# A streaming encoder step on one core: the sample's value products beside the first prompt rows', other buffers and addresses for some weights, other column chunks

## The chip, the cores and the metric

The kernel runs on one core of a Trainium2 chip. Its engines are PE (matrix products; PEld is its weight load), DVE (vector), ACT (scalar, with activation functions), POOL (GpSimd) and SP (issues transfers). On-chip memory is SBUF; matrix products are accumulated in banks of PSUM. The time is microseconds (us) of one execution on the device. Lines such as L1385 are those of the kernel before; below the change they move by a few.

## What is computed

One inference step of an encoder layer, in float32, for 1024 prompt rows and 64 sample rows (the sample also has 512 cached rows of keys and values). One projection of width 6144 gives queries, keys, values and a gate z for two branches of eight heads of 64 each, and two output gates. The first branch ("sb") is stick-breaking attention, the second ("cb") softmax attention in a band with a relative bias. Cut to that:

```python
h = rms_norm(x, norm_w) @ w_in
sb_q, sb_k, sb_v, sb_z, cb_q, cb_k, cb_v, cb_z, g_sb, g_cb = jnp.split(h, SPLIT_POINTS, axis=-1)
# stick-breaking: suffix sums of log(1 - beta) over the keys behind
suffix = lax.cumsum(log_keep, axis=3, reverse=True) - log_keep
w = jnp.where(causal, jnp.exp(log_beta + suffix), 0.0)
o_sb = jnp.einsum("bhqk,bkhd->bqhd", w, v)
# band: keys of the own chunk of 64 and the eight before it
o_cb = softmax(q @ k * ATTN_SCALE + bias) @ v
b_sb = (o_sb * jax.nn.silu(sb_z)) @ w_proj_sb
b_cb = (o_cb * jax.nn.silu(cb_z)) @ w_proj_cb
y = x + (jax.nn.sigmoid(g_sb) * b_sb + jax.nn.sigmoid(g_cb) * b_cb) @ w_out
```

Prompt and sample go through the same formulas; y and the new keys and values of both are returned.

## The kernel before

Every float32 factor is split in two parts, high (rounded) and low (the rest), and a product is made of three: high by high, high by low, low by high. Where blocks of weights are multiplied with blocks of x, a scheme of seven products of sums in place of eight products is used on top of that. The order of all instructions is written out by hand (manual_schedule): each engine takes its own in program order, and semaphores that the framework sets between tiles make one engine wait for another. A tile of a pool with bufs=2 may be taken again only when all users of the tile two before are done.

The stages, one after another on PE:

- Natural products (L528, 11 to 177 us): six blocks of 256 columns, nine row tiles each. The weights of a half block are whi and wlo (pool wpool) or whix and wlox (pool natx); x and the sums of x are xa, xm, xb. In between DVE makes four sums of x, t0 to t3, each with a high and a low part (tiles t0h, t0l and so on) in jobs, one at each place (block, tile) of the list jobs_at; the operations are at L189. open_t allots t0 and t1 in the pool tp0, t2 and t3 in the pool tp2; pad puts unused bytes behind one of them. POOL and DVE also normalise and store; hl at L375 is the low part of transposed keys, for which PE's transposes pk at L370 wait.
- Pairs (L868, 218.6 to 516.1 us): 14 pairs of column blocks, each in seven steps s = 0 to 6 of 24 products into one of three banks for two chunks c of columns (256 and 288). The operands of a step are t0 to t3 or x, and a weight block that prep(n + LEAD), five steps before, has cast to its high part on ACT (L456) and whose low part POOL has made. Results are joined on DVE at L876 (u2, u3), L880 and L888 and emitted; s1 at L872 is ACT's copy of the first. A bank is written again only after DVE has read it. In pairs 0 and 2 keys are made: PE transposes them (L787, into acc) and ACT copies them out (ko, kos, L790 to L799); pairs 1 and 3 make queries (emitted by ACT as hl at L765, by DVE at L766).
- Units (run_fill, L1037): the output gates' columns, four plain units with three chunks of columns, 1088 in all (CH); they run from 516.1 us, and their rest and the projection of the first branch (L1144) fill gaps of the attention.
- Attention (540 to 812 us): eight passes (b, p), two heads each. A pass goes over t = 8 (the sample), 0, 1, ..., 7 (row tiles of 128). qk makes z = q k (L1293); for "sb" ACT takes the sigmoid (L1296) and DVE a scan (mid, L1315), for "cb" DVE adds the bias and takes a minimum (L1298) and ACT the exponential (L1306) and the scaling (L1318). Four rows of the sequence later tr transposes (L1346, pt), ACT or DVE copies to wT (L1355, L1357), and av(b, p, j) multiplies wT by the values into the PSUM tile o (L1385): vp for prompt rows, j = 0 to 3 (256 rows), vs for the sample, j = 4. Then DVE reads o and multiplies by the gate tile zt (L1394 for "sb", L1396 for "cb"), and POOL stores zt an iteration later. The pool of o has one buffer. The list avq holds when av is due.
- Branch and output projections (L1186, L1705, to 958 us).

The two places of the attention loop that set when av comes:

```python
        while avq and avq[0][0] <= i:
            av(*avq.pop(0)[1:])
...
            if t == 8 or hd == 1 and t % 2 == 1:
                avq.append((i + (3 if t == 8 else 2), b, p, t // 2 if t < 8 else 4))
```

Of the kernel before, what the change touches and what calls it, by code (L numbers as in the profile page):

```python
# [8 lines left out]
F32 = mybir.dt.float32  # L9
F32R = mybir.dt.float32r  # L10
# [23 lines left out]
def hybrid_step_kernel(ctx: ExitStack, tc: tile.TileContext, x_prompt, x_sample, c_sbk, c_sbv, c_cbk, c_cbv,  # L34
# [80 lines left out]
    class Weights:  # L115
# [18 lines left out]
        def lo(self, key, eng=None):  # L134
            raw, pool, shape, extra = self.raw.pop(key)
            h = self.sp[key][0]
            l = shifted(pool, shape, 1) if extra else pool.tile(shape, F32R, name="wlo", bufs=2)
            (eng or G).tensor_tensor(out=l, in0=raw, in1=h[:].bitcast(F32), op=OP.subtract)
            self.sp[key] = (h, l)
# [74 lines left out]
    with ExitStack() as ph:  # L214
# [219 lines left out]
        def prep(n):  # L434
# [14 lines left out]
            shape = [128, 2, 4, 128]  # L449
            if s in (0, 3):  # L450
                t = shifted(natx, shape, 1)
            elif s in (2, 4):
                t = natx.tile(shape, F32R, name="whix", bufs=2)
            else:
                t = wpool.tile(shape, F32R, name="whi" if s == 5 else "wlo", bufs=2)
            A.activation(t[:, 0], src, AF.Copy)  # L456
# [72 lines left out]
        tms = [None] * 4  # L529
        jobs_at = [(2, 0), (2, 3), (2, 6), (3, 0), (3, 4), (3, 7), (4, 1), (4, 4)]  # L530

        rb_at = [(1, 0), (1, 1), (1, 3), (1, 4), (1, 6), (1, 7), (2, 0), (2, 1)]

        def open_t(ns):
            tp = sx.enter_context(tc.tile_pool(name=f"tp{ns[0]}", bufs=1, side="right"))
            for n in ns:
                tms[n] = [tp.tile([128, 4, XO], F32R, name=f"t{n}{s}") for s in "hl"]
            if ns[0] == 0:
                pad(tp, 128)
# [463 lines left out]
    def ev_act(func, dst, ci, a, b, ps):  # L1003
        n = b - a
        sg = am.tile([128, 384], F32, name="sg", bufs=3)
        A.activation(sg[:, :n], ps[:, :n], func)
        for o, n0, m in pieces(a, b):
            store_later(dst[:, n0:n0 + m], sg[:, o:o + m])
# [21 lines left out]
    def run_fill():  # L1030
        for j, (kind, c, args) in enumerate(units):
            wh, wl = W.sp.pop(("u", j))
            for ci, (a, b) in enumerate(CH):
                ps = psF.tile([128, 512], F32, name="acc")
# [331 lines left out]
    def av(b, p, j):  # L1366
        o = psO.tile([128, 256], F32, name="o")
        vp, vs = VP[b, p]
# [89 lines left out]
    for i in range(len(seq) + LAG + 2):  # L1458
# [34 lines left out]
        if 0 <= i - LAG < len(seq):  # L1493
            tr(i - LAG)
            b, p, t, hd = seq[i - LAG]
            if t == 8 or hd == 1 and t % 2 == 1:
                avq.append((i + (3 if t == 8 else 2), b, p, t // 2 if t < 8 else 4))
        fill(m - m // 2)
# [299 lines left out]
```

## Time and profile before

| | |
|---|---|
| median of three runs | 962.02 us (960.46 to 962.95) |
| the profiled execution | 960.25 us |
| its span | 958.5 us, TensorE clock 0.999 |
| busy PE / DVE / ACT / POOL | 951.5 / 589.8 / 499.9 / 394.0 us |
| pairs, 218.6 to 516.1 us: PE / DVE / ACT | 297.49 / 134.98 / 115.10 us |
| "sb" passes, 540 to 655 us: PE / DVE / ACT | 114.78 / 94.43 / 81.71 us |
| "cb" passes, 655 to 812 us: PE / DVE / ACT | 156.62 / 110.69 / 117.79 us |

Busy is the time in which an engine executes. In the timeline rows shown below the first number is the start within the span, the second the duration from there, then engine, line, operation, the output tile, "<-" and the inputs, the shape, and the count of alike instructions that the row groups (x20). Successive products of PE overlap in such rows, since they are pipelined: what one costs is the distance of starts. Brackets at the end give idle time of the engine ahead of the row and what ended it. A row of PE's waits names who waited, for what, and the total, the count and the longest in us.

### The profile page before, as it was taken

The page shows a single profiled execution, that of the slowest core. Times are in us where ns is not written, and L with a number is a line of the kernel's source. Part 1 is how long each engine was busy: PE and PEld are TensorE (multiplying, and loading weights), DVE is VectorE, ACT ScalarE, POOL GpSimd, SP SyncE. Part 2 cuts the span into 40 slices and gives each one's busy share as a digit, 9 for nine tenths or more (in the row PEclk, how much of TensorE's full clock was granted, in tenths as well). Part 3 has the DMA queues.
Part 4 walks back from the last instruction along what each step waited for, and adds up shares of the span by engine and source line. Part 5 has one row for each costly group of instructions (what it writes and reads, how often), then busy time and mean ns, then how long its engine had stood idle before and what let it go on. Part 6 is the DMA issues. An engine that isn't in the chain of part 4 may idle for free.

```text
span 958.5 us, 20551 instructions
## 1 busy us (share of the span) xinstructions
PE 951.5 (99%) x7595; PEld 904.9 (94%) x7595; DVE 589.8 (62%) x1156; ACT 499.9 (52%) x1159; POOL 394.0 (41%) x393
## 2 busy tenths in 40 slices
PE   9999999999999999999999999999999999999998
PEld 8999999999999999999999987888988888999998
DVE  6656674974454554533332389777777875499735
ACT  6566775333444433343432376767886874456220
POOL 3266664245444566655542100111331012676641
PEclk9999999999999999999999999999999999999999
DMA  6736756235656555555434997768899933852742
GB/s 226 246 130 250 264 202 209 68 118 168 192 178 195 156 185 169 160 175 179 146 90 120 271 249 207 195 188 229 240 291 248 246 97 102 258 176 74 225 138 75
DMA packets 173498, 175.77 MB, mean 183 GB/s; under 512 B 30922, under 2 KB 157710, under 8 KB 173271
## 3 DMA queue, kind: packets, MB, share of 16 engines
q1 hardware_dynamic: 162102, 159.58, 56.1%
q10 hardware_dynamic: 8608, 8.20, 2.6%
q0 software_dynamic: 2688, 6.69, 2.2%
q8 instruction: 60, 0.98, 0.4%
q14 instruction: 40, 0.32, 0.1%
HBM read 112.42 MB, written 62.00 MB: 182 GB/s over the span
## 4 chain that ended last, share of the span: by engine, by line
PE 91%; DVE 5%; issue 2%; ACT 1%; POOL 1%; DMA 1%; ACTq 0%; DVEq 0%; POOLq 0%
PE b L868 30%; PE acc L528 14%; PE o L1385 7%; PE z L1293 7%; PE pt L1346 7%; PE b L1705 6%; PE acc L1144 5%; PE acc L1037 5%; PE b L704 3%; PE b L1186 2%; DVE acc L1231 1%; DVE tk L1228 1%; PE pk L370 1%; PE pt L301 1%; DVE b L1191 1%
## 5 line engine op out<-in xcount | busy, mean ns | idle before, releaser
L1346 PE MATMUL pt<-ident,be 128*128 128x128 f32 (+1 forms) x568 | 87.7, 278 | 0.6 <-ACT wT L1355 0.4
L1315 DVE TENSOR_TENSOR_SCAN be<-be,imp 128x128 f32<-128x128 f32 (+7 forms) x64 | 83.4, 1343 | 8.0 <-ACT be L1296 7.7
L1293 PE MATMUL z<-ks,sq 128*128 128x320 f32 (+5 forms) x384 | 87.4, 338 | 0.0
L1355 ACT ACTIVATE wT<-pt 128x512 f32<-128x512 f32 (+3 forms) x123 | 56.9, 496 | 42.9 <-PE pt L1346 42.8
L1346 PEld LDWEIGHTS pt<-ident,be 128*128 128x128 f32 (+1 forms) x568 | 65.7, 140 | 13.2 <-issue 4.6
L868 PE MATMUL b<-xm,wlox 128*128 128x256 f32 (+1 forms) x336 | 76.0, 286 | 0.0
L876 DVE TENSOR_TENSOR u<-b,s 128x256 f32<-128x256 f32 (+1 forms) x56 | 24.4, 440 | 75.2 <-PE b L868 69.7
L1293 PEld LDWEIGHTS z<-ks,sq 128*128 128x128 f32 x384 | 63.7, 190 | 1.7
L1385 PE MATMUL o<-wT,vp 128*64 128x256 f32 (+1 forms) x608 | 64.2, 356 | 0.0
L1385 PEld LDWEIGHTS o<-wT,vp 128*64 128x64 f32 x608 | 40.3, 136 | 23.7 <-issue 7.6
L868 PEld LDWEIGHTS b<-xm,wlox 128*128 128x128 f32 x336 | 56.8, 188 | 0.0
L1318 ACT ACTIVATE be<-be,sm 128x640 f32<-128x640 f32 (+5 forms) x68 | 47.2, 694 | 17.3 <-DVE sm L1317 17.2
L941 POOL DMA_DIRECT2D d_osb<-zt x20 | 10.8, 540 | 103.2 <-DVE zt L1394 67.2
L528 PE MATMUL acc<-whi,xa 128*128 128x256 f32 x192 | 52.8, 294 | 0.0
L457 POOL TENSOR_TENSOR whix<-ws,whix 128x512 fp32r<-128x512 f32 x28 | 36.6, 1306 | 32.9 <-ACT whix L456 29.5
L528 PE MATMUL acc<-whix,xb 128*128 128x256 f32 x192 | 50.1, 280 | 0.0
L528 PE MATMUL acc<-wlox,xm 128*128 128x256 f32 x192 | 50.1, 281 | 0.0
L528 PE MATMUL acc<-whix,xm 128*128 128x256 f32 x192 | 49.9, 279 | 0.0
L1306 ACT ACTIVATE be<-be,sm 128x640 f32<-128x640 f32 (+5 forms) x68 | 47.3, 695 | 4.9 <-DVE sm L1298 4.5
L528 PE MATMUL acc<-whi,xm 128*128 128x256 f32 x192 | 49.8, 279 | 0.0
L528 PE MATMUL acc<-wlo,xa 128*128 128x256 f32 x192 | 49.7, 278 | 0.0
L1296 ACT ACTIVATE be<-z 128x384 f32<-128x384 f32 (+6 forms) x104 | 47.9, 515 | 3.1 <-PE z L1293 2.1
(379 smaller groups left out, 3248.4 us busy)
## 6 DMA issues: line engine op xcount, KB each, us to landing
wraw<-in_w_in_dram SPq DMA_DIRECT2D x31, 512.0 KB, 4.5
wrawx<-in_w_in_dram SPq DMA_DIRECT2D x16, 512.0 KB, 5.8
sq<-d_qsbT SPq DMA_DIRECT2D x32, 192.0 KB, 5.8
sq<-d_qcbT SPq DMA_DIRECT2D x32, 192.0 KB, 5.2
xt<-in_x_prompt_dram SPq DMA_DIRECT2D x8, 512.0 KB
d_kcbT<-hl SPq DMA_DIRECT2D x8, 512.0 KB, 5.7
d_qcbT<-hl SPq DMA_DIRECT2D x8, 512.0 KB, 4.6
ks<-d_ksbT SPq DMA_DIRECT2D x16, 256.0 KB, 6.0
```

The source lines that it names most:

```text
L528: TE.matmul(ps, x, w, start=first, stop=last)
L868: TE.matmul(ps[:, :m], w[:, hl_, k], right[s](x)[:, k, a:b], start=s < 3 and k == 0 and e == 0, stop=k == 3 and e == 2, skip_group_check=s ...
L1037: TE.matmul(ps[:, :b - a], w[:, k], xk(x, k)[:, a:b], start=k == 0 and n == 0, stop=k == KT - 1 and n == 2)
L1144: TE.matmul(ps[:, :e - a], w[:, p, cw], g[:, a:e], start=m % 12 == 0, stop=m % 12 == 11)
L1293: TE.matmul(z[:, :m], s[:, e, q0:q0 + 128], ks[:, h, o + x:o + y], start=(e, h) == parts[0], stop=(e, h) == parts[-1])
L1296: A.activation(be[:r, x:y], z[:r, :m], AF.Sigmoid, scale=-0.125)
L1306: A.activation(be[:, :n], be[:, :n], AF.Exp, bias=kp[:, j:j + 1], scale=-1.0, accum_out=kp[:, 2:3])
L1315: V.tensor_tensor_scan(be[:r, n - 1::-1], be[:r, n - 1::-1], im[:, ::-1], 0.0, op0=OP.mult, op1=OP.max)
L1346: TE.transpose(pt[:kr, x, :r], be[:r, kb * 128:kb * 128 + kr], ident[:r, :r])
L1355: A.activation(w[:, sl:sl + m, q0:q0 + r], pt[:, :m, :r], AF.Copy)
L1385: TE.matmul(o[hd * 64:hd * 64 + 64, c0:c1], vv[:kr, kb, hd * 64:hd * 64 + 64], wT[b, p, j, hd, s // 4][:kr, s % 4, c0:c1] if j < 4 else wT ...
L1705: TE.matmul(ps[:, t], left[s](xs_, k)[:, ts_], wt_[:, k], start=s < 3 and t == k == e == 0, stop=k == 3 and e == 2, skip_group_check=s > 2 ...
```

## The change

It does these things:

- av of the sample (j = 4) comes six in place of three iterations after its transposes, which is right ahead of av of j = 0, and both use one PSUM tile o, 512 wide: j = 0 columns 0 to 255, the sample columns 256 to 319.
- The weight block of step 5 of each pair is a tile "wlox" of natx, as those of steps 0 and 3 are, in place of a tile "whi" of wpool.
- 128 unused bytes are allotted in the pool of t2 and t3 too.
- The natural weights' low parts in natx (wlox) begin 128 bytes on, or no longer on, by turns: the other parity.
- The first job on the sums comes at the last tile of block 1 in place of the first of block 2.
- The chunks of the plain units are 448, 384 and 256 columns in place of 384, 384 and 320, and the staging tile sg is 448 wide.

The order of instructions at three places, with the waits that an instruction has (49 is a counter's name). DVE in the second "sb" pass, around the sample's instruction zt<-o,vl,zt 128x64, before:

```order
L1394 SCALAR_TENSOR_TENSOR zt<-o,vl,zt 128x128 [waits DMAHW1_49,DMASW3_49,PE_49]
L1394 SCALAR_TENSOR_TENSOR zt<-o,vl,zt 128x128
L1315 SCALAR_TENSOR_TENSOR be<-be,imp 128x384 [waits Activation_49] x2
L1394 SCALAR_TENSOR_TENSOR zt<-o,vl,zt 128x64 [waits DMAHW5_49,DMASW4_49,PE_49]
L1315 SCALAR_TENSOR_TENSOR be<-be,imp 128x512 [waits Activation_49] x2
L1315 SCALAR_TENSOR_TENSOR be<-be,imp 128x640 [waits DVE_49,Activation_49]
L1394 SCALAR_TENSOR_TENSOR zt<-o,vl,zt 128x128 [waits DMAHW6_49,DMASW5_49,PE_49]
L1394 SCALAR_TENSOR_TENSOR zt<-o,vl,zt 128x128
L1315 SCALAR_TENSOR_TENSOR be<-be,imp 128x640 [waits DVE_49,Activation_49]
```

and in the change:

```order
L1399 SCALAR_TENSOR_TENSOR zt<-o,vl,zt 128x128 [waits DMAHW1_49,DMASW3_49,PE_49]
L1399 SCALAR_TENSOR_TENSOR zt<-o,vl,zt 128x128
L1315 SCALAR_TENSOR_TENSOR be<-be,imp 128x384 [waits Activation_49] x2
L1315 SCALAR_TENSOR_TENSOR be<-be,imp 128x512 [waits Activation_49] x2
L1315 SCALAR_TENSOR_TENSOR be<-be,imp 128x640 [waits DVE_49,Activation_49]
L1399 SCALAR_TENSOR_TENSOR zt<-o,vl,zt 128x64 [waits DMAHW5_49,DMASW4_49,PE_49]
L1399 SCALAR_TENSOR_TENSOR zt<-o,vl,zt 128x128 [waits DMAHW6_49,DMASW5_49,PE_49]
L1399 SCALAR_TENSOR_TENSOR zt<-o,vl,zt 128x128
L1315 SCALAR_TENSOR_TENSOR be<-be,imp 128x640 [waits DVE_49,Activation_49]
```

The sample's row has moved behind the three scans (128x512 twice and 128x640) and stands right ahead of those of j = 0. PE in the same pass, up to the products of j = 0 (vp; the sample's are vs), before:

```order
L1346 MATMUL pt<-ident,be 128x128 [waits DVE_49,Activation_49]
L1346 MATMUL pt<-ident,be 128x128 x2
L1293 MATMUL z<-ks,sq_7883 128x320 [waits Activation_49]
L1293 MATMUL z<-ks,sq_7883 128x320
L1293 MATMUL z<-ks,sq_7883 128x320 [waits Activation_49]
L1293 MATMUL z<-ks,sq_7883 128x320
L1385 MATMUL o<-wT,vp 64x256 [waits DMAHW2_49,DVE_49]
L1385 MATMUL o<-wT,vp 64x256
L1385 MATMUL o<-wT,vp 64x128 x2
L1346 MATMUL pt<-ident,be 128x128 [waits PE_49]
L1346 MATMUL pt<-ident,be 128x128 x2
```

and in the change:

```order
L1293 MATMUL z<-ks,sq_7883 128x320 [waits Activation_49]
L1293 MATMUL z<-ks,sq_7883 128x320
L1293 MATMUL z<-ks,sq_7883 128x320 [waits Activation_49]
L1293 MATMUL z<-ks,sq_7883 128x320
L1390 MATMUL o<-wT,vs 64x64 [waits DMAHW3_49]
L1390 MATMUL o<-wT,vs 64x64 x7
L1390 MATMUL o<-wT,vs 64x64 [waits DMAHW4_49]
L1390 MATMUL o<-wT,vs 64x64
L1390 MATMUL o<-wT,vp 64x256 [waits DMAHW2_49,DVE_49]
L1390 MATMUL o<-wT,vp 64x256
L1390 MATMUL o<-wT,vp 64x128 x2
L1346 MATMUL pt<-ident,be 128x128 [waits PE_49]
```

The sample's products now stand between the z products and those of j = 0. The wait on DVE at the first vp row was there before; the DVE instruction that it means is in both cases the one that read o last, which in the change is the sample's own. ACT at the start of the pairs (casts of weight blocks at L456, s and hl copies of the steps' results), before:

```order
L456 ACTIVATE whi<-wraw 128x512
L872 ACTIVATE s_3386<-b_3373 128x256 [waits DMAHW3_49,DMAHW4_49,DMAHW2_49,DMAHW5_49,DMAHW1_49,DMAHW6_49,DMAHW0_49,DMAHW7_49,PE_49,Activation_49]
L872 ACTIVATE s_3401<-b_3388 128x288 [waits PE_49]
L456 ACTIVATE wlo<-ws 128x512 [waits DVE_49]
L456 ACTIVATE wlox<-wrawx 128x512 [waits DMAHW1_49,Pool_49]
L456 ACTIVATE wlo<-ws 128x512 [waits DVE_49,PE_49]
L765 ACTIVATE hl<-b_3373 128x256 [waits PE_49]
L765 ACTIVATE hl<-b_3388 128x288 [waits PE_49]
L456 ACTIVATE whix<-ws 128x512 [waits Pool_49]
L765 ACTIVATE hl<-u_3526 128x256 [waits DVE_49]
L765 ACTIVATE hl<-u_3540 128x288 [waits DVE_49]
L456 ACTIVATE wlox<-wraw 128x512 [waits DMAHW2_49,Pool_49]
```

and in the change:

```order
L456 ACTIVATE wlox<-wraw 128x512 [waits PE_49,Pool_49]
L872 ACTIVATE s_3387<-b_3374 128x256 [waits DMAHW4_49,DMAHW5_49,DMAHW3_49,DMAHW6_49,DMAHW2_49,DMAHW7_49,DMAHW1_49,DMAHW0_49]
L872 ACTIVATE s_3402<-b_3389 128x288
L456 ACTIVATE wlo<-ws 128x512 [waits DVE_49]
L456 ACTIVATE wlox<-wrawx 128x512 [waits DMAHW1_49,PE_49,Pool_49]
L456 ACTIVATE wlo<-ws 128x512 [waits DVE_49]
L765 ACTIVATE hl<-b_3374 128x256
L765 ACTIVATE hl<-b_3389 128x288
L456 ACTIVATE whix<-ws 128x512
L765 ACTIVATE hl<-u_3527 128x256 [waits DVE_49]
L765 ACTIVATE hl<-u_3541 128x288 [waits DVE_49]
L456 ACTIVATE wlox<-wraw 128x512 [waits DMAHW2_49,PE_49,Pool_49]
```

The order is the same; the first, the fifth and the last row, casts into wlox, have got a wait on PE.

The diff:

```diff
--- before.py
+++ after.py
@@ -134,7 +134,7 @@
         def lo(self, key, eng=None):
             raw, pool, shape, extra = self.raw.pop(key)
             h = self.sp[key][0]
-            l = shifted(pool, shape, 1) if extra else pool.tile(shape, F32R, name="wlo", bufs=2)
+            l = shifted(pool, shape, 0) if extra else pool.tile(shape, F32R, name="wlo", bufs=2)
             (eng or G).tensor_tensor(out=l, in0=raw, in1=h[:].bitcast(F32), op=OP.subtract)
             self.sp[key] = (h, l)
 
@@ -447,12 +447,12 @@
             else:
                 src = sums[{1: 2, 2: 1, 4: 3, 6: 4}[s]]
             shape = [128, 2, 4, 128]
-            if s in (0, 3):
+            if s in (0, 3, 5):
                 t = shifted(natx, shape, 1)
             elif s in (2, 4):
                 t = natx.tile(shape, F32R, name="whix", bufs=2)
             else:
-                t = wpool.tile(shape, F32R, name="whi" if s == 5 else "wlo", bufs=2)
+                t = wpool.tile(shape, F32R, name="wlo", bufs=2)
             A.activation(t[:, 0], src, AF.Copy)
             G.tensor_tensor(out=t[:, 1], in0=src, in1=t[:, 0].bitcast(F32), op=OP.subtract)
             blk[n] = t
@@ -527,7 +527,7 @@
             x = xs[:, k] if t == 8 else xk(n % 2, k)[:, xc(t):xc(t) + rows(t)]
             TE.matmul(ps, x, w, start=first, stop=last)
         tms = [None] * 4
-        jobs_at = [(2, 0), (2, 3), (2, 6), (3, 0), (3, 4), (3, 7), (4, 1), (4, 4)]
+        jobs_at = [(1, 8), (2, 3), (2, 6), (3, 0), (3, 4), (3, 7), (4, 1), (4, 4)]
 
         rb_at = [(1, 0), (1, 1), (1, 3), (1, 4), (1, 6), (1, 7), (2, 0), (2, 1)]
 
@@ -535,7 +535,7 @@
             tp = sx.enter_context(tc.tile_pool(name=f"tp{ns[0]}", bufs=1, side="right"))
             for n in ns:
                 tms[n] = [tp.tile([128, 4, XO], F32R, name=f"t{n}{s}") for s in "hl"]
-            if ns[0] == 0:
+            if ns[0] in (0, 3):
                 pad(tp, 128)
 
         for i in range(nb):
@@ -1002,7 +1002,7 @@
 
     def ev_act(func, dst, ci, a, b, ps):
         n = b - a
-        sg = am.tile([128, 384], F32, name="sg", bufs=3)
+        sg = am.tile([128, 448], F32, name="sg", bufs=3)
         A.activation(sg[:, :n], ps[:, :n], func)
         for o, n0, m in pieces(a, b):
             store_later(dst[:, n0:n0 + m], sg[:, o:o + m])
@@ -1030,7 +1030,7 @@
     def run_fill():
         for j, (kind, c, args) in enumerate(units):
             wh, wl = W.sp.pop(("u", j))
-            for ci, (a, b) in enumerate(CH):
+            for ci, (a, b) in enumerate(((0, 448), (448, 832), (832, T))):
                 ps = psF.tile([128, 512], F32, name="acc")
                 for k in range(KT):
                     for n, (w, x) in enumerate(((wh, 0), (wh, 1), (wl, 0))):
@@ -1364,7 +1364,12 @@
         zts[b, p, j] = zt
 
     def av(b, p, j):
-        o = psO.tile([128, 256], F32, name="o")
+        o = late.pop("o5", None) if j == 0 else None
+        if o is None:
+            o = psO.tile([128, 512], F32, name="o")
+        if j == 4:
+            late["o5"] = o
+            o = o[:, 256:320]
         vp, vs = VP[b, p]
         if j == 4:
             nq = 64
@@ -1494,7 +1499,7 @@
             tr(i - LAG)
             b, p, t, hd = seq[i - LAG]
             if t == 8 or hd == 1 and t % 2 == 1:
-                avq.append((i + (3 if t == 8 else 2), b, p, t // 2 if t < 8 else 4))
+                avq.append((i + (6 if t == 8 else 2), b, p, t // 2 if t < 8 else 4))
         fill(m - m // 2)
     flush(True)
     yst.close()
```

## The prediction

> **What bounds the kernel now.** I read the page's busy times first, then its chain, then the waits of PE.
>
> ```profile
> PE 951.5 (99%) x7595; PEld 904.9 (94%) x7595; DVE 589.8 (62%) x1156; ACT 499.9 (52%) x1159; POOL 394.0 (41%) x393
> ...
> PE 91%; DVE 5%; issue 2%; ACT 1%; POOL 1%; DMA 1%; ACTq 0%; DVEq 0%; POOLq 0%
> ...
> PE pk L370 <- DVE hl L375: 0.5, 1, 0.5
> ```
>
> PE is busy for 951.5 of 958.5 us and makes up 91% of the chain that ended last; its longest wait on another engine's data inside the work, at L370, is 0.5 us. So PE is the bound in every stage, and two things alone can move the time: how long PE's own instructions take, and new waits of PE. DVE, ACT and POOL have room on average, but PE's order is fixed: a stall of PE isn't made up later, because there is no later wait to shorten. The number of products and their columns stay the same in all parts.
>
> **The sample's products joined to the first prompt rows'.** In each of the eight passes (four stick-breaking, four band) the sample's 20 products now stand right ahead of the products of j = 0, both in one PSUM tile o. The program's order gives the first product of j = 0 a wait on DVE, and the DVE instruction that it waits for is now the sample's own, which reads o. Before, that instruction was long done. The second pass, first PE and then DVE (start, duration, engine, line, operation):
>
> ```profile
> 578.41 0.95 PE L1385 MATMUL o<-wT,vs 128*64 128x64 f32 x20
> 579.28 0.44 PE L1346 MATMUL pt<-ident,be 128*128 128x128 f32 x2
> ...
> 581.98 0.87 PE L1385 MATMUL o<-wT,vp 128*64 128x256 f32 x8
> ...
> 577.85 1.80 DVE L1315 TENSOR_TENSOR_SCAN be<-be,imp 128x384 f32<-128x384 f32 x2
> 579.57 0.26 DVE L1394 SCALAR_TENSOR_TENSOR zt<-o,vl,zt 128x64 f32<-128x64 f32 x1
> 579.74 3.73 DVE L1315 TENSOR_TENSOR_SCAN be<-be,imp 128x512 f32<-128x512 f32 x3
> 583.39 0.59 DVE L1394 SCALAR_TENSOR_TENSOR zt<-o,vl,zt 128x128 f32<-128x128 f32 x2
> ...
> 609.40 3.72 DVE L1315 TENSOR_TENSOR_SCAN be<-be,imp 128x512 f32<-128x512 f32 x3
> ```
>
> The sample's DVE instruction (579.57) moves behind the three scans that follow it, since DVE takes them in program order. DVE is busy without a gap from 577.85 to 583.47 (579.74 + 3.73). Without the sample's slot of 0.17 (579.57 to 579.74) the scans end at 583.30; the sample's instruction is then overlapped as it is now (the 583.39 row starts 0.08 before the scans end), so it starts at 583.22, ends 0.26 later at 583.48, and j = 0 starts about 0.05 after that, at 583.53. Before it started at 581.98. This is +1.55, whatever PE does ahead of it: the sample's block holds PE for 0.87 (578.41 to 579.28), so PE is back at its old place 0.87 earlier, puts the sample's products there, and then waits. The 609.40 row shows the same three scans in the third pass. The sample's store, which POOL issues an iteration after that instruction, goes out later too; nothing on PE reads it before the passes are over, so I cost it at nothing. 4 x 1.55 = **+6.2**. If DVE is free instead, PE waits for 0.95 (the block to its end) + 0.05 + 0.26 + 0.05 = 1.31 where the block cost 0.87: +0.44, less some 0.1 for the one change into o that is saved, so +0.3. That is the lower end; nothing lies below it while the wait stands on the sample's own instruction. The upper end, a scan 0.2 later, is +1.75.
>
> In the band passes DVE has no scans; here it is the reductions of L1298 and the multiplication of L1396:
>
> ```profile
> 677.74 0.87 PE L1385 MATMUL o<-wT,vp 128*64 128x256 f32 x8
> ...
> 677.96 0.55 DVE L1298 CUSTOM_DVE_ANT_0 be<-z,bias,sm 128x320 f32<-128x320 f32 x1
> 678.43 0.08 DVE L1298 DVE_READ_ACCUMULATOR2_ANT sm<- 128x1 f32 x1
> 678.65 0.42 DVE L1396 TENSOR_TENSOR zt<-o,zt 128x256 f32<-128x256 f32 x1
> ```
>
> The last reduction ahead of L1396 ends at 678.51 (678.43 + 0.08), 0.1 before PE's products. PE reaches the place 0.87 earlier than now. If the reductions come 0.87 earlier with it, since z comes earlier too, DVE is free: +0.3. If they stay, the sample's instruction (0.26 as at 579.57) ends at 678.77 and j = 0 starts at 678.82 instead of 677.74: +1.1. I take 0.6, a little nearer the free end, because the reductions follow PE's z: 4 x 0.6 = **+2.4** (1.2 to 4.4). What is late next in both kinds of pass is PE's transposes and z products of the next rows; they and everything behind them shift by the whole stall.
>
> **Weight block 5 of each pair in natx "wlox" instead of wpool "whi".** Two buffers now serve blocks 0, 3 and 5, so a block's cast on ACT (L456) must wait until PE has finished the step two blocks back in this row. Blocks are cast five steps ahead: in step 0 block 5, which waits for the end of step 0; in step 2 block 0 of the next pair, which waits for the end of step 3; in step 5 its block 3, which waits for the end of step 5. ACT takes its queue in order, so what stands behind is late too. In the program's order each of these casts has got a wait on PE. GpSimd's subtraction for the same block follows the cast and is needed only five steps later. Two places decide. A q pair (ACT, then DVE, then PE):
>
> ```profile
> 248.52 0.62 ACT L456 ACTIVATE wlox<-wraw 128x512 fp32r<-128x512 f32 x1
> 249.04 0.25 ACT L790 ACTIVATE kos<-acc 32x128 f32<-32x128 f32 x1
> ...
> 249.67 0.36 ACT L799 ACTIVATE ko<-acc 128x256 f32<-128x256 f32 x1
> 251.03 0.63 ACT L456 ACTIVATE wlo<-ws 128x512 fp32r<-128x512 f32 x1 [1.00 <-DVE ws L422]
> 254.28 0.41 ACT L765 ACTIVATE hl<-b 128x288 fp32r<-128x288 f32 x1 [1.21 <-PE b L868]
> ...
> 255.65 0.42 DVE L876 TENSOR_TENSOR u<-b,s 128x256 f32<-128x256 f32 x1 [0.47 <-PE b L868]
> ...
> 257.05 0.28 PE L868 MATMUL b<-t3h,whi 128*128 128x256 f32 x1
> ```
>
> The cast at 248.52 now waits for the end of step 3, which released the hl at 254.28. Behind it in ACT's order stand five small copies (0.25 each and overlapping, from 249.04 to 250.03: about 0.9), the cast of 251.03 (0.63) and both hl; with the cast's own 0.62 the hl of 254.28 ends near 257.0 (254.28 + 0.62 + 0.9 + 0.63, and some 0.6 for two overlapping hl of 0.4). DVE then takes its own difference on it (0.4) and only then the sum u of 255.65 (0.42), which ends near 257.8. Step 5 accumulates into the bank that this sum reads, and PE comes there at 257.05: a stall of 0.8, x 2 q pairs = **+1.6**. A k pair (ACT, then PE):
>
> ```profile
> 280.65 0.62 ACT L456 ACTIVATE wlox<-wraw 128x512 fp32r<-128x512 f32 x1
> ...
> 281.59 0.36 ACT L799 ACTIVATE ko<-acc 128x256 f32<-128x256 f32 x1
> ...
> 281.59 0.96 PE L787 MATMUL acc<-ident,u 128*128 128x128 f32 x6
> 282.31 0.37 PE L868 MATMUL b<-xm,wlo 128*128 128x256 f32 x1
> ```
>
> The cast at 280.65 now waits for the end of step 5, about 281.55, since PE's next instruction starts at 281.59. The copies behind it (as at 281.59, 0.36 each) empty the acc buffers that the transposes at 281.59 fill, so these wait some 1.15 (281.55 + 0.62 + 0.36 + 0.15 for the hand-over and a part of a second copy, against 281.59). With 0.2 at step 5's own start: 1.35 x 2 = **+2.7**. In the ten pairs without transposes ACT has few copies; I take 0 there (the margin by the same working is about 0.1 in the silu pairs). Together **+4.3**, from +1 (ACT's delay mostly absorbed) to +9 (0.5 in each of the other ten).
>
> **128 bytes ahead of the fourth sum.** Three like steps of 24 products, by their starts; the fourth row is the next step:
>
> ```profile
> 307.53 0.28 PE L868 MATMUL b<-xa,wlox 128*128 128x256 f32 x1
> ...
> 310.49 0.28 PE L868 MATMUL b<-t1h,wlo 128*128 128x256 f32 x1
> ...
> 313.45 0.28 PE L868 MATMUL b<-t0h,whix 128*128 128x256 f32 x1
> ...
> 316.47 0.28 PE L868 MATMUL b<-xm,wlox 128*128 128x256 f32 x1
> ```
>
> The xa and t1 steps take 2.96, the t0 step 3.02. I expect the t3 steps, whose operands stand alike, to run as the t0 step. If the new addresses of t3 and its weights bring it to 2.96, that is 14 x 0.06 = −0.8; if not, 0. I take **−0.5**.
>
> **The low weights of the natural tiles, other parity** (first products' half, second half, next tile):
>
> ```profile
> 43.93 0.28 PE L528 MATMUL acc<-whi,xa 128*128 128x256 f32 x1
> ...
> 45.31 0.28 PE L528 MATMUL acc<-whix,xm 128*128 128x256 f32 x1
> ...
> 46.71 0.28 PE L528 MATMUL acc<-whi,xa 128*128 128x256 f32 x1
> ```
>
> The half with wlox takes 1.40, the other 1.38. 48 such halves x 0.02 = **−0.9** (0 to −1.3).
>
> The Trainium skill speaks against both parts: "SBUF — State Buffer", section "SBUF: two separate sides", has contention only on the port that GpSimd and VectorE share and on the AXI ports, with PE never waiting on anyone. By it an address is worth nothing, and both terms would be 0. The rows above, 3.02 beside 2.96 for the same count and columns, speak for a small effect, but not that the address is its cause.
>
> **A DVE job earlier.**
>
> ```profile
> 73.39 0.72 DVE L189 TENSOR_TENSOR d<-xa 128x544 f32<-128x544 f32 x1
> 74.15 1.48 DVE L189 TENSOR_TENSOR d<-d,xm 128x544 f32<-128x544 f32 x2
> 75.55 0.42 DVE L375 TENSOR_TENSOR hl<-pk,hl 128x256 fp32r<-128x256 f32 x1
> ```
>
> The job (73.39 to 75.63) holds back the hl at 75.55, for which PE waits 0.47 (the 0.5 in the waits above). Moved ahead into a gap of DVE it gives **−0.45** (0 to −0.47).
>
> **Units in 448, 384, 256 columns.**
>
> ```profile
> 516.06 0.33 PE L1037 MATMUL acc<-xa,whi 128*128 128x384 f32 x1
> ...
> 520.21 0.34 PE L1037 MATMUL acc<-xa,whi 128*128 128x384 f32 x1
> ...
> 524.37 0.31 PE L1037 MATMUL acc<-xa,whi 128*128 128x320 f32 x1
> ...
> 527.89 0.34 PE L1037 MATMUL acc<-xa,whi 128*128 128x384 f32 x1
> ```
>
> 24 products of 384 take 4.16, of 320 3.52: 26.7 ns for each 64 columns more. So 448 would take 4.80, and 256, by the 1.38 of 12 products above, 2.76: 4.80 + 4.16 + 2.76 = 11.72 against 4.16 + 4.16 + 3.52 = 11.84. 4 units x −0.1 = **−0.4** (+0.1 to −0.7). The stores are as many as before.
>
> The sum is 6.2 + 2.4 + 4.3 − 0.5 − 0.9 − 0.45 − 0.4 = +10.65. The profiled execution took 960.25 and would take 970.9; the median of the runs shown, 1.77 higher, goes to 962.02 + 10.65 = **972.7**.
>
> **Rivals.**
> - *The waits cost only their hand-over* (not slower). DVE reaches the sample's instruction when its products end, because ACT and with it the scans are ahead of PE: 8 x 0.3 = 2.4, and ACT's casts are absorbed: 2.4 − 2.25 = +0.15, 962.2; with addresses at their best ends a little under. It decides if DVE is idle when the sample's products end. For it speaks DVE's 62%; against it the unbroken 577.85 to 583.47. Faster by 0.3% (2.9 us, about what a measurement can tell from no change) needs besides that the pool tiles moved by the wider staging tile run better, for which I have no row.
> - *DVE free at the join, ACT's waits real*: 2.4 + 4.3 − 2.25 = +4.45, 966.5.
> - *Join as priced, ACT's waits hidden*: 6.2 + 2.4 − 2.25 = +6.35, 968.4. For it: ACT's 52%.
> - *ACT's wait cascades into the other ten pairs*, 0.5 each: +15.65, 977.7.
> - *Addresses are worth nothing* (the page's rule): without −0.5 and −0.9, +12.05, 974.1.
>
> **Chances.** My forecast 0.38; hand-over only 0.20; DVE free 0.13; ACT hidden 0.19; cascade 0.06; addresses nothing 0.04. Of the 0.20 I give 0.13 to within 0.3% and 0.07 to faster; the rest, 0.80, is slower by over 0.3%. My forecast's own range is 969 to 976. The range to hold 8 in 10 leaves out the cascade's top and most of the hand-over case: 964 to 977.
>
> **What the profile after would show.** PE's waits: o <- DVE zt eight times, some 1.5 in the stick-breaking passes and 0.3 to 1 in the band passes; b <- DVE u about 0.8 at step 5 of two pairs; acc <- ACT ko about 1.1 in two. The wait of pk for hl is gone, t3 steps fall to 2.96. I am wrong if PE waits for o under 0.5 in the first four passes, or if there is no wait on ACT in the pairs.

## The result, and the profile after

The changed kernel takes 973.21 us (median of four runs, 971.83 to 974.33); the kernel before took 962.49 in the same comparison. The ratio is 1.0115, with a 95% interval of 1.0095 to 1.0135: slower, by 10.7 us at the medians. A second comparison, later and on another chip than most of the experiments below, gave 974.14 against 961.79, a ratio of 1.0127 (1.0111 to 1.0143), or 12.4 us. The profiled execution took 973.37, its span is 971.6, against 958.5 before: 13.1 more. That is more than between the medians, since the profiled execution of the kernel before (960.25) lies 2.2 under its median and that of the change does not.

Busy times on the page of the changed kernel:

```profile
PE 950.9 (98%) x7595; PEld 903.0 (93%) x7595; DVE 593.3 (61%) x1156; ACT 496.2 (51%) x1159; POOL 392.7 (40%) x393
```

PE has as much to do as before (951.5 there), in a span that is 13.1 longer. The loss is waiting. PE's waits (who, for what, total, count, longest):

```profile
PE o L1390 <- DVE zt L1399: 5.8, 4, 1.5
PE b L868 <- DVE u L876: 2.5, 3, 1.2
PE acc L787 <- ACT ko L799: 2.1, 2, 1.1
PE o L1390 <- DVE zt L1401: 1.7, 4, 0.7
...
PE pt L392 <- DMA ck<-in_cache_sb_k_dram: 0.5, 1, 0.5
```

Of the waits that have no counterpart before, the first four hold 12.1 us: the joins of the stick-breaking passes (o, L1399), the pairs (u and acc), the joins of the band passes (o, L1401). The wait of pk for hl (0.5 before) is gone; a new one, of pt at L392 for a transfer, has its size. Two more are new: 1.1 at L301, ahead of the natural products, which begin at 9.70 all the same (9.63 before), and 0.4 at L1710, in the output projection.

The join in the second pass, PE and then DVE; the rows to set beside it are those at 578.41 to 583.39 before:

```profile
587.56 0.95 PE L1390 MATMUL o<-wT,vs 128*64 128x64 f32 x20
590.02 0.87 PE L1390 MATMUL o<-wT,vp 128*64 128x256 f32 x8 [1.51 <-DVE zt L1399]
...
584.38 5.41 DVE L1315 TENSOR_TENSOR_SCAN be<-be,imp 128x384 f32<-128x384 f32 x5
589.71 0.26 DVE L1399 SCALAR_TENSOR_TENSOR zt<-o,vl,zt 128x64 f32<-128x64 f32 x1
590.94 0.61 DVE L1399 SCALAR_TENSOR_TENSOR zt<-o,vl,zt 128x128 f32<-128x128 f32 x2 [0.97 <-PE o L1390]
```

The sample's products end at 588.51 (587.56 + 0.95). DVE is in its scans until 589.79 (584.38 + 5.41), takes the sample's instruction to 589.97, and PE goes on at 590.02. In the band passes DVE is mostly free at that place:

```profile
687.58 0.95 PE L1390 MATMUL o<-wT,vs 128*64 128x64 f32 x20
688.86 0.87 PE L1390 MATMUL o<-wT,vp 128*64 128x256 f32 x8 [0.33 <-DVE zt L1401]
...
688.58 0.22 DVE L1401 TENSOR_TENSOR zt<-o,zt 128x64 f32<-128x64 f32 x1 [0.26 <-PE o L1390]
```

Here the wait is the bare hand-over: the products end at 688.53, DVE takes 0.22 from 688.58, and PE starts at 688.86.

In the pairs, the q pair (ACT, then DVE, then PE):

```profile
254.82 0.63 ACT L456 ACTIVATE wlox<-wraw 128x512 fp32r<-128x512 f32 x1 [6.49 <-PE b L868]
...
256.25 0.61 ACT L456 ACTIVATE wlo<-ws 128x512 fp32r<-128x512 f32 x1
256.77 0.65 ACT L765 ACTIVATE hl<-b 128x256 fp32r<-128x256 f32 x2
...
257.87 0.78 DVE L876 TENSOR_TENSOR u<-b,s 128x256 f32<-128x256 f32 x2
...
258.33 0.38 PE L868 MATMUL b<-t3h,wlox 128*128 128x256 f32 x1 [0.65 <-DVE u L876]
```

ACT stands still for 6.49 us in front of the cast, with all that is behind it; the sum u comes at 257.87, and PE's step 5 waits for it. In the k pair (ACT, then PE) the transposes wait for the copy behind the cast:

```profile
283.21 0.63 ACT L456 ACTIVATE wlox<-wraw 128x512 fp32r<-128x512 f32 x1 [0.85 <-PE b L868]
...
284.16 0.96 PE L787 MATMUL acc<-ident,u 128*128 128x128 f32 x6 [1.05 <-ACT ko L799]
```

And pair 4, the first whose result goes through a sigmoid, which the prediction had at nothing:

```profile
323.11 0.63 ACT L456 ACTIVATE wlox<-wraw 128x512 fp32r<-128x512 f32 x1 [5.85 <-PE b L868]
323.65 0.62 ACT L456 ACTIVATE wlo<-ws 128x512 fp32r<-128x512 f32 x1
324.29 1.28 ACT L759 ACT_TABLE_LOAD   x1
325.58 0.69 ACT L759 ACTIVATE hl<-b 128x256 f32<-128x256 f32 x2
...
327.17 0.38 PE L868 MATMUL b<-t3h,wlox 128*128 128x256 f32 x1 [1.19 <-DVE u L876]
```

The same place before:

```profile
314.14 0.61 ACT L456 ACTIVATE wlox<-wraw 128x512 fp32r<-128x512 f32 x1
...
317.74 1.28 ACT L759 ACT_TABLE_LOAD   x1
```

The table of the sigmoid is loaded where it is first used. Before, the cast was done long ahead of the load, and PE took pair 4 without a wait. Now the load stands behind the late cast and adds its 1.28 to the same chain.

By the starts of the first products of each stage in the two traces, the differences (after less before) in us are: start and natural products −0.8; pairs 0 to 4 +1.2, +0.9, +1.2, +0.9, +1.4; pairs 5 to 13 together −0.3; units −0.1; attention +7.4; projections and end +1.3. The last also differs between executions of kernels whose projections are alike (−0.9 to +2.3 in the kernels below; −0.6 in the second trace of the changed kernel itself), so the 1.3 is not shown to belong to the change.

### The profile page after: what moved, and what is told of

It reads as the page before. It is cut to its first block, busy times and chain, and to the rows that moved or that the text cites. A ratio compares the mean times of both kernels' runs of the same rounds, so it can differ in the third digit from the quotient of the medians.

```text
span 971.6 us, 20475 instructions
## 1 busy us (share of the span) xinstructions
PE 950.9 (98%) x7595; PEld 903.0 (93%) x7595; DVE 593.3 (61%) x1156; ACT 496.2 (51%) x1159; POOL 392.7 (40%) x393
## 4 chain that ended last, share of the span: by engine, by line
PE 56%; DVE 4%; DMA 2%; issue 1%; SPq 1%; ACT 1%; ACTq 0%; DVEq 0%
PE b L868 20%; PE o L1390 7%; PE pt L1346 6%; PE b L1710 6%; PE z L1293 6%; PE acc L1144 5%; PE b L1186 4%; PE acc L1037 2%; DMA ks<-d_ksbT 1%; SPq L52 1%; DMA sq<-d_qsbT 1%; DVE acc L1231 1%; DVE be L1315 1%; PE acc L1753 1%; DVE tk L1228 1%
## 5 line engine op out<-in xcount | busy, mean ns | idle before, releaser
L457 POOL TENSOR_TENSOR wlox<-wraw,wlox 128x512 fp32r<-128x512 f32 x29 | 40.0, 1379 | 81.0 <-ACT wlox L456 78.1
L1318 ACT ACTIVATE be<-be,sm 128x640 f32<-128x640 f32 (+5 forms) x68 | 47.2, 694 | 18.8 <-DVE sm L1317 18.6
L456 ACT ACTIVATE wlox<-wraw 128x512 fp32r<-128x512 f32 x29 | 18.2, 628 | 63.3 <-PE b L868 51.6
```

The lines of the kernel that those rows point to most:

```text
L457: G.tensor_tensor(out=t[:, 1], in0=src, in1=t[:, 0].bitcast(F32), op=OP.subtract)
L1318: A.activation(be[:r, :n], be[:r, :n], AF.Copy, scale=kp[:r, 3:4])
```

## The experiments

### The join undone

```diff
-        o = late.pop("o5", None) if j == 0 else None
-        if o is None:
-            o = psO.tile([128, 512], F32, name="o")
-        if j == 4:
-            late["o5"] = o
-            o = o[:, 256:320]
+        o = psO.tile([128, 256], F32, name="o")
...
-                avq.append((i + (6 if t == 8 else 2), b, p, t // 2 if t < 8 else 4))
+                avq.append((i + (3 if t == 8 else 2), b, p, t // 2 if t < 8 else 4))
```

> The change, with the sample's products back three iterations after their transposes and in a PSUM tile of their own; all else as changed. Theory (each join makes PE wait for the sample's own DVE instruction, which stands behind a scan): the waits of PE for o (5.8 in the stick-breaking passes, 1.7 in the band passes) are gone, and the time falls by 6.5 to 7.5, to about 966. Rival (the two-fold join costs only its hand-over, and the rest of PE's wait would come elsewhere, at the transposes): the time falls by 2.4 at most, to 971 or more, with new waits of PE for wT or be.

Measured: 965.98 us against 961.39, a ratio of 1.005 (1.0035 to 1.0065). Set beside the change's 1.0115, that is 6.2 us gone; between the medians it is 7.2. PE's waits:

```profile
PE b L868 <- DVE u L876: 2.5, 3, 1.2
PE acc L787 <- ACT ko L799: 2.1, 2, 1.1
```

No wait for o is left and none has come instead; those for u and acc are as in the change. The attention takes 282.7 us here (from the first z product to the first at L1186), 289.8 in the change and 282.4 before: the join costs 7.1, of it 5.75 in the four stick-breaking passes and 1.35 in the four band passes. The theory holds; the time agrees with what it said (6.5 to 7.5) by the medians and falls a little short of it by the ratios.

### The block of step 5 back in wpool

```diff
-            if s in (0, 3, 5):
+            if s in (0, 3):
                 t = shifted(natx, shape, 1)
...
-                t = wpool.tile(shape, F32R, name="wlo", bufs=2)
+                t = wpool.tile(shape, F32R, name="whi" if s == 5 else "wlo", bufs=2)
```

> The change, with the weight block of step 5 back in wpool; all else as changed. Theory (ACT's casts wait for PE, and what stands behind them is late): the waits of PE for u and for acc in pairs 0 to 4 are gone, the 14 pairs take what they took before less 0.05 each, and the time falls by 5.5 to 6.0, to about 967.5. Rival (ACT's waits are hidden and the pairs are slower for the addresses of the block): the steps' own lengths would fall, and the waits stay.

Measured: 968.64 us (965.11 to 971.0), a ratio of 1.0074 (1.0049 to 1.01). PE's waits:

```profile
PE o L1390 <- DVE zt L1399: 5.8, 4, 1.5
PE o L1390 <- DVE zt L1401: 1.7, 4, 0.7
```

The waits for u and for the copies ko are gone, and the 14 pairs take 0.5 more than before instead of 5.35; the 0.5 stands in pair 0 (below). So the pairs agree with the theory but for pair 0, and each of the last ten is 0.02 shorter than before, not 0.05. The time fell by less than it said, about 4 us, with runs that are 6 apart: their mean granted clock was 0.999 in the run of 965.11 and 0.997 in that of 971.0, which the experiment on the clock takes up.

### The scan behind the join

```diff
-        if 0 < i <= len(seq) and seq[i - 1][0] == "sb":
+        first = bool(avq) and avq[0][0] <= i and avq[0][3] == 4
+        if 0 < i <= len(seq) and seq[i - 1][0] == "sb" and not first:
             mid(i - 1)
...
             av(*avq.pop(0)[1:])
+        if 0 < i <= len(seq) and seq[i - 1][0] == "sb" and first:
+            mid(i - 1)
```

> The change, with DVE's scan of the iteration in which the join stands issued behind the sample's and the first prompt rows' DVE instructions instead of ahead of them, in the four stick-breaking passes; PE's order is the same. Theory (the wait of 1.4 is a queue on DVE, with a hand-over of 0.5 at its base): PE's wait for o falls to about 0.3 to 0.4 in each of the four passes, and the time by about 4 x 1.1 = 4.4, to 969, if no transposes wait for the late scan; if those wait, less. Rival (PE's wait is the price of two users of one PSUM bank, whatever DVE has to do): the wait stays at 1.4 and the time at 973.

Measured: 969.36 us, a ratio of 1.0086 (1.0067 to 1.0106). PE in the second pass, and DVE:

```profile
587.36 0.95 PE L1390 MATMUL o<-wT,vs 128*64 128x64 f32 x20
588.69 0.87 PE L1390 MATMUL o<-wT,vp 128*64 128x256 f32 x8 [0.39 <-DVE zt L1399]
...
588.35 0.28 DVE L1399 SCALAR_TENSOR_TENSOR zt<-o,vl,zt 128x64 f32<-128x64 f32 x1
```

The wait is 0.39 where it was 1.51, the four together 1.5 instead of 5.8, and the attention takes 285.6, 4.15 less than in the change. No new wait of the transposes has come. So some three quarters of the join's price in these passes is DVE's queue. The rest, 0.39 a pass, is the way from PE to DVE and back, with DVE free; the band passes have 0.33 for it.

### The same order, nothing shared

```diff
-        o = late.pop("o5", None) if j == 0 else None
-        if o is None:
-            o = psO.tile([128, 512], F32, name="o")
-        if j == 4:
-            late["o5"] = o
-            o = o[:, 256:320]
+        o = psO.tile([128, 256], F32, name="o")
```

> The change, with the sample's products joined as changed but in a PSUM tile of their own from the same one-buffer pool, so that nothing is shared. Theory (it is the order and the one buffer that make PE wait, not that two users share a tile): the waits of PE for o stay at 5.8 and 1.7, and the time at that of the change, 972 to 973. Rival (the shared tile causes them): the waits go, and the time falls to about 966.

Measured: 974.02 us, a ratio of 1.013 (1.0116 to 1.0143).

```profile
PE o L1385 <- DVE zt L1394: 5.8, 4, 1.5
...
PE o L1385 <- DVE zt L1396: 1.7, 4, 0.7
```

The waits are those of the change to the tenth. The shared tile is not the cause: two users that stand one behind the other in a pool with one buffer wait for each other's reader, shared or not.

### Two banks for o

```diff
-    psZ = att.enter_context(tc.tile_pool(name="az", bufs=3, space=PS))
+    psZ = att.enter_context(tc.tile_pool(name="az", bufs=2, space=PS))
-    psO = att.enter_context(tc.tile_pool(name="ao", bufs=1, space=PS))
+    psO = att.enter_context(tc.tile_pool(name="ao", bufs=2, space=PS))
```

The tile o is 512 wide and not shared here, and step 5's block is in wpool.

> The sample's products joined to those of j = 0 as in the change, but in separate PSUM banks (two buffers for o; the z products have two in place of three), and the weight block of step 5 back in wpool. Theory (the wait at the join is only the reuse of o): no wait of PE for o, the sample's block costs 0.2 to 0.3 less in each pass than with its own place, so about 2 under the kernel without the join if z can do with two buffers; z with two buffers makes PE wait for ACT's or DVE's reading instead, which I expect to cost more than that, 2 to 20. Rival (joined products of different banks wait as well): the waits for o stay at 1.4.

Measured: 964.5 us, a ratio of 1.0033 (1.002 to 1.0046). PE has no wait for o:

```profile
581.78 0.95 PE L1385 MATMUL o<-wT,vs 128*64 128x64 f32 x20
582.65 0.87 PE L1385 MATMUL o<-wT,vp 128*64 128x256 f32 x8
```

j = 0 starts 0.87 after the sample, as any next work did before. The z products pay for it: their 160 products of 320 columns stand 184.0 ns apart at the mean instead of 156.4 (sums of the distances of starts), 4.4 us in all. All that stands outside of z takes as long as in the kernel with neither wait (below). So the saving of 0.2 to 0.3 a pass that I expected of the join itself is not there: at most 0.1, in the step from the last product ahead of the sample's to the sample's (0.24 instead of 0.33 in the stick-breaking passes). What the join could have won was too small to pay for any wait.

### The sigmoid's table loaded early

```diff
+                if (i, s) == (4, 2):
+                    A.activation(warm[:, 0:1], ident[:, 0:1], AF.Sigmoid)
                 prep(n + LEAD)
```

> The change, with one more ACT instruction, a sigmoid of one column into unused bytes, ahead of step 2 of pair 4, which loads the table of the sigmoid while ACT has nothing to do. Theory (pair 4 loses 1.35 at step 4 because the table's load of 1.29 stands behind ACT's cast that waits for the end of step 3): the load comes at step 1 or 2, step 4 of pair 4 takes 2.96 to 3.1 instead of 4.31, and the time falls by 1.2 to 1.35. Rival (the late cast itself holds step 4): step 4 stays at 4.3, and the time at 973.

ACT around pair 4's steps 2 to 4:

```profile
317.00 1.28 ACT L852 ACT_TABLE_LOAD   x1
...
322.94 0.63 ACT L456 ACTIVATE wlox<-wraw 128x512 fp32r<-128x512 f32 x1 [4.45 <-PE b L870]
...
324.00 0.67 ACT L759 ACTIVATE hl<-b 128x256 f32<-128x256 f32 x2
```

The load lies at 317.00, where ACT waits anyway, the two hl come 1.3 earlier behind the cast, and pair 4 takes what it took before (20.84 instead of 22.27): in the trace the theory holds. The time does not show it: 972.88 us, a ratio of 1.012 (1.0105 to 1.0135), as in the change. In the profiled execution two things take the gain back: a stretch of low clock behind the second join, which the change's first trace has not and which costs 1.6, and pair 7, 0.5 longer, where PE waits 0.21 for DVE. What hid the gain in the other three executions is not shown.

### A longer wait at the join

The runs of the four experiments whose joins make PE wait lay 2.9 to 5.9 apart, those of the join undone and of the two banks 1.6 and 2.3 (four runs each), and only among the former are mean clocks of 0.997 and 0.998. The change once more, and a kernel that makes DVE later at the four joins:

```diff
+        if avq and avq[0][0] <= i and avq[0][1] == "sb" and avq[0][3] == 4:
+            for _ in range(2):
+                V.tensor_tensor(out=imp[:, 0:896], in0=imp[:, 0:896], in1=imp[:, 0:896], op=OP.max)
         while avq and avq[0][0] <= i:
```

> The changed kernel once more, beside the next kernel. Three earlier kernels with joins show, right behind one of the joins, some 3 us in which the granted clock of PE is about 0.55, and the kernels without joins show none inside the work. Theory (the clock falls after a wait of PE, in some executions): 972 to 974, the runs with a mean clock of 0.998 about 1 us longer than those with 1.000. Rival (chance of the chip): no relation.

> The change, with two more DVE instructions ahead of the sample's in the four stick-breaking passes (a maximum of a tile with itself, 128 x 896, which leaves its values as they are); PE has nothing more to do. Theory (PE waits for DVE's queue at the join, and a wait of PE brings the clock down for about 3 us in some cases, at 1.6 each): each of the two instructions takes 1.0, the waits for o grow from 1.45 to 3.4, the time by 4 x 1.95 = 7.8 for the waits and 2 to 6 more for the clock, to 982 to 987, with granted clocks near 0.5 behind two or more of the four joins. Rival (the clock has nothing to do with the waits): 980.5 to 981, and no more low clocks than in the change.

The change: 974.14 us (972.9 to 975.3), mean clocks 0.997 to 0.998; the two runs at 0.997 are not longer than the two at 0.998 (973.05 and 975.22 against 972.9 and 975.3), so that finer part of the theory is not shown. Its profile has one low stretch, behind the third join. The columns are the stretch of time, its length, busy times of PE, PEld, DVE, ACT and POOL, PE's granted clock, the share of DMA and GB/s:

```profile
618.00:620.00 2.00, 1.64 (x24) 1.04 (x22) 2.00 (x3) 1.52 (x5) 0.00 (x0) 1.00 0.26 73
620.00:622.00 2.00, 0.84 (x6) 0.58 (x8) 1.11 (x2) 0.00 (x0) 0.49 (x1) 0.86 0.17 38
622.00:624.00 2.00, 2.00 (x12) 1.67 (x9) 1.47 (x3) 0.49 (x1) 0.52 (x2) 0.50 0.79 216
624.00:626.00 2.00, 2.00 (x12) 1.87 (x12) 1.06 (x2) 1.54 (x4) 0.08 (x1) 0.79 1.00 269
...
621.16 1.11 PE L1390 MATMUL o<-wT,vp 128*64 128x256 f32 x6 [1.52 <-DVE zt L1399]
```

PE waits for 1.52 to 621.16, and from there the clock is at half for some 3.4 us; that pass loses 1.6 more than its neighbours. With the longer wait: 989.07 us, a ratio of 1.0279 (1.0262 to 1.0297), more than either theory said. Each of the two added instructions took 1.09. The waits grew to 14.9 in all (3.6 to 3.8 each), 9.1 more than in the change, and the median by 14.9: 5.8 us are more than the waits. One window behind each of the four joins:

```profile
564.00:566.00 2.00, 1.22 (x8) 0.77 (x8) 0.73 (x2) 0.00 (x0) 0.54 (x1) 0.50 0.87 212
...
602.00:604.00 2.00, 2.00 (x10) 1.91 (x9) 1.92 (x3) 0.95 (x2) 0.54 (x1) 0.50 0.13 30
...
636.00:638.00 2.00, 2.00 (x12) 1.29 (x11) 0.66 (x3) 0.00 (x0) 0.55 (x1) 0.50 1.00 230
...
674.00:676.00 2.00, 2.00 (x9) 1.90 (x8) 1.38 (x2) 1.36 (x3) 1.14 (x5) 0.50 1.06 276
```

All four lengthened joins are followed by a half clock, and so is a wait of 1.8 in pair 0 of this execution. Behind the four joins it costs 1.5 to 2.9 each, 8.5 in all in this execution (the longest of the four), by the lengths of the passes beside the change's first trace, less what the waits grew. The five traces with waits of 1.3 to 1.5 at the joins (the change twice, step 5's block back, nothing shared, the table early) have 20 of them, and four are followed by a half clock, one in each trace but the change's first. In the other traces (before, the join undone, the scan behind, the two banks, and the two below) the clock falls nowhere but in the last few us.

The traces show more of what decides. In each of the twelve, all changes of the granted clock lie whole multiples of 3.41 us apart. Cut the work on this grid into stretches of 3.41. Five stretches in which PE was busy for at most 0.42 of the time, all in the kernel with the longer wait, were each followed by the half clock. Of twelve with 0.55 to 0.60, four were; of those above 0.60, none. Two such stretches of the change's second trace:

```profile
587.27:590.69 3.42, 1.90 (x30) 1.27 (x29) 2.65 (x3) 1.06 (x4) 0.36 (x1) 1.00 0.31 74
617.99:621.40 3.41, 1.89 (x26) 1.24 (x26) 3.12 (x4) 1.53 (x5) 0.00 (x0) 1.00 0.22 58
```

PE is busy for 0.55 of both, and only the second is followed by the half clock; what parts these two is not shown. Where the grid cuts a wait of 1.5 in two, both stretches can stay above 0.60. So a wait of PE costs its own length, and some 1.5 to 2.9 more where it empties enough of one stretch. One of 23 runs of the kernel before, in a later comparison, took 964.81 with a mean clock of 0.998; it has no trace, so a fall without a join is not ruled out.

The Trainium skill, "TensorE: Matmul & The Clock Gate", section "HAM oscillation — how this bites in real kernels", has the clock halve when PE idles for more than about 3.4 us. The halving agrees with these rows, and the waits of 3.6 to 3.8 us were each followed by it; the bound does not hold as a safe one here, since a wait of 1.4 to 1.5 us was followed by it in four of the five traces that have such waits.

### The four small parts alone, and without the addresses

The first kernel has both undoings above (the join and step 5's block) and keeps the rest of the change; the second has these two lines undone besides:

```diff
-            l = shifted(pool, shape, 0) if extra else pool.tile(shape, F32R, name="wlo", bufs=2)
+            l = shifted(pool, shape, 1) if extra else pool.tile(shape, F32R, name="wlo", bufs=2)
...
-            if ns[0] in (0, 3):
+            if ns[0] == 0:
```

> The change without its two waits: the sample's products back in their place with a PSUM tile of their own, and the weight block of step 5 back in wpool; the other four parts as changed. Theory (the loss is these two parts, and the others gain what the stages of the changed kernel's trace show: 1.0 in the natural products, 0.02 to 0.05 a pair, 0.1 in the units): 1 to 2 faster than before, about 960, and no wait of PE over 0.5 in the pairs or the attention. Rival (the parts need each other, so that the addresses of step 5's block carry the gain): no faster than before, with steps 5 at 3.0.

> The kernel without its two waits, and with the two address parts undone as well (other parity of wlox, 128 bytes at t3): only the earlier job and the chunks of the units are left. Theory (the address matters to PE): the products wlox by xm take 125 ns from start to start again, in place of 118.5, and the time is 1.0 to 1.5 above that of the kernel with them, about 961.5. Rival (addresses are worth nothing, the 1.3 came from elsewhere): 118.5 and no difference.

Measured: the first 960.59 us, a ratio of 0.9989 (0.9979 to 0.9999); the second 961.3, a ratio of 0.9996 (0.9985 to 1.0006). The first is the fastest kernel of this study, by about 1 us of 961 by the ratio and 0.5 between the medians, at the edge of what these runs can tell; the second is no different from before. The two differ by 0.7 between their medians, where 1.0 to 1.5 was expected, and their intervals overlap. A half tile with wlox, first kernel and then second:

```profile
44.81 0.28 PE L528 MATMUL acc<-whix,xm 128*128 128x256 f32 x1
...
46.17 0.28 PE L528 MATMUL acc<-whi,xa 128*128 128x256 f32 x1
```

```profile
45.10 0.28 PE L528 MATMUL acc<-whix,xm 128*128 128x256 f32 x1
...
46.51 0.28 PE L528 MATMUL acc<-whi,xa 128*128 128x256 f32 x1
```

1.36 against 1.41: the address does matter to PE, in this block of columns; in others the difference is smaller. Over the 192 products wlox by xm the mean distance of starts is 118.6 ns in the first and 121.3 in the second, 0.5 us in all. Without the products that another line follows it is 116.1 to 116.4 in the ten traces with the new addresses and 118.9 in both with the old ones, so this is not chance. The 125 that I expected had PE's wait of 0.47 at L370 in it, which follows such a product. Some of what is gained goes again further on. In pair 0, the first kernel's PE waits at L787 for kf, which DVE makes behind a sum of weights that have to be fetched first. DVE in that pair, first kernel:

```profile
228.66 1.04 DVE L422 TENSOR_TENSOR ws<-wrawx,wraw 128x512 f32<-128x512 f32 x1 [4.14 <-DMA wraw<-in_w_in_dram]
```

That pair takes 0.5 to 1.0 more than before in the three kernels with step 5's block back and the new addresses (0.5, 0.65 and 0.96) and 1.8 in the one without the addresses, whose PE came there hardly earlier than before (218.39 and 218.56); and it took 24.09 and 24.63 in the two traces of the changed kernel. So it seems to be the transfer's own time in an execution that sets it. That PE being early makes it worse is plausible, but was not tried.

## Why the prediction was right, and where not

The time, 973.21, lies 0.5 from the 972.7 predicted, and the two waits that were to make it are there, at their places and released by the engines named. That the number came so close is in part luck: the second comparison has the change cost 12.4, 1.7 more than the sum, and the terms err both ways:

- **The join in the stick-breaking passes**: +6.2 forecast, +5.75 measured (change against the join undone). The working from DVE's queue holds: 1.44 a pass instead of 1.55.
- **The join in the band passes**: +2.4 forecast, +1.35 measured. Three of the four waits were the bare hand-over (0.33 the one shown), one 0.70, with a reduction of L1298 still ahead on DVE. The step that failed is the choice of 0.6 between 0.3 and 1.1: the reductions did move ahead with PE, as z came earlier.
- **Step 5's block**: +4.3 forecast for pairs 0 to 3, +4.2 measured (1.24 and 1.17 in the k pairs against 1.35, 0.88 and 0.90 in the q pairs against 0.8). But pair 4 costs another 1.4. There the step "I take 0 in the ten pairs without transposes" failed: the margin of 0.1 said for the silu pairs leaves out that the first one has the load of the sigmoid's table (1.28) in the same queue of ACT. Before, it was hidden ahead of PE's need.
- **128 bytes at t3**: −0.5 forecast, −0.3 measured. The bytes stand in a pool that holds t3 alone, not t2 and t3 as said above. Pairs 8 to 13 take 0.05 less each than before, 0.3 in all, and pairs 5 to 7 next to nothing less; with step 5's block back in wpool it is 0.02 a pair. So 0.02 of the 0.05 come without the block's new place; what the new place does without the bytes was not tried. The step itself, in pair 8 of the change, from its first product to the first of step 6:

```profile
410.67 0.28 PE L868 MATMUL b<-t3h,wlox 128*128 128x256 f32 x1
...
413.63 0.28 PE L868 MATMUL b<-xm,wlo 128*128 128x256 f32 x1
```

It takes 2.96, as said.

- **The parity of wlox**: −0.9 forecast, −0.5 measured by the products themselves. The rule weighed against these two terms, that addresses are worth nothing, is not borne out (116.1 to 116.4 against 118.9 ns above), though what they are worth is near what the times can tell.
- **The DVE job**: the wait of 0.47 is gone as forecast, and in the change's profile PE, then earlier, waits 0.45 at L392 for a transfer that has not landed. In the trace with the join undone that wait isn't there. The gain is real but is given back in some executions.
- **The units**: −0.4 forecast, 0.0 measured: the sum of the distances of starts behind the products of L1037 is the same in both traces. The step that failed is the price of 256 columns, taken from another stage's products: 24 of them take 2.83 here, not 2.76, while 448 take the 4.80 forecast.
- **Not in the prediction**: the half clock behind a wait, 1.6 a time in some executions (not in the change's first trace), and the +1.3 behind the attention in that trace.

The sum came out near because errors of both signs met: less for the band passes (−1.05) and the stick-breaking ones (−0.45), no gain in the units (+0.4), half of that of wlox (+0.4), less of t3 (+0.2), the DVE job's gain given back (+0.45) and pair 4 (+1.4). That adds up to 12.0. The stages up to the end of the attention take 11.8 more, and the projections behind them 1.3: the 13.1 between the two spans.

## What to carry to other kernels

When PE is the bound, putting two users of a one-buffer PSUM pool one behind the other puts the reader's engine on PE's path: look up what stands in that engine's queue ahead of the reader, since this, more than the reader's own length, was what PE waited for here (1.51 with a scan ahead, 0.39 without). A cast that is given a buffer with a later release holds up its whole queue; follow what stands behind it, the table load that comes once included. And price a wait of PE above its own length, since the clock may fall behind it, and the more surely the more of one 3.41 us stretch the wait takes.

## What had not been expected of the hardware

In a stream of products that keeps PE 98% busy, four of 20 waits of 1.3 to 1.5 us were followed by 3.41 us at half the granted clock, 1.6 us lost, and waits of 3.6 to 3.8 were in four of four cases, for 3.41 or 6.83 us. The clock changed on a grid of 3.41 us alone, and inside the work it never fell behind a stretch of it in which PE was busy for more than 0.60 of the time. Putting the sample's products right ahead of those of j = 0 saved at most 0.1 us a time. The sigmoid's table load took 1.28 us on ACT, and the instructions on both sides of it followed within 0.02.
